# Order of the first loads, and early loads of the later x tiles, in a one-core transformer block

## The chip, the cores and the metric

The kernel runs on one core of a Trainium2 chip. The metric is the time of one execution in device microseconds; the smaller the better. The engines are named as in the profile: PE is TensorE's matrix multiplication and PEld its weight load, DVE is VectorE, ACT is ScalarE, POOL is GpSimd, and SP is the engine that issues nearly all transfers.

## The reference, cut to what matters

One block of a transformer over 1024 tokens of width 1024, in float32:

```python
x = x + _hybrid_mixer(_rms_norm(x, norm1_g), w_in, ...)      # two kinds of sparse attention
x = x + _memory_xattn(_rms_norm(x, norm2_g), mem, ...)       # cross attention over 256 memory rows
x = x + _sq_relu_mlp(_rms_norm(x, norm3_g), w_ff_in, w_ff_out)

def _rms_norm(x, g):
    return x * rsqrt(mean(x * x, axis=-1) + 1e-6) * g

# at the start of _hybrid_mixer, h being the normalised x
proj = h @ w_in                       # 1024 x 1760
c_q, c_kv, k_idx, w_idx, q_nsa, kv_nsa, g_nsa = split(proj)
q_d = rope(rms_norm(rms_norm(c_q) @ w_dsa_uq));  q_i = rope(rms_norm(c_q) @ w_idx_q)
k_d, v_d = split(rms_norm(c_kv) @ w_dsa_ukv)     # keys are normalised and rotated too
```

From `kv_nsa` come keys and values of three branches, one of them compressed over blocks of 32 tokens. The queries then attend, 128 at a time, to the top 256 keys of an index score, to compressed blocks, to selected blocks and to a window of 512.

## The kernel before, in words

Tokens are handled in eight tiles of 128 rows. `PARTS` makes two parts of them, tiles one to four and tiles five to eight. The **head** projects part 0 (`project(p1, 0, ...)`): each tile of x is loaded, normalised and transposed by `norm_T` (square on ACT with the sum of squares, a reciprocal root on DVE and POOL, the scaling by root and gain on DVE at line 290, the transposes on PE at line 277 into PSUM, evacuation by ACT and DVE), and then the columns of `w_in` are worked through in chunks of 256 by `gemm`. In the head x and the weights are split into a high and a low half, so that one product takes three matmuls (`load_w`, `split_w`; line 221 is the helper that issues a matmul). In the second part one float32 matmul takes their place (`load_whole`, line 268). `compress` makes the compressed keys and values. `k_prep` normalises and rotates the keys and transposes them (lines 460 to 480). `stage_q` copies projected queries from PSUM into a staging tile and stores them to DRAM (lines 404 and 406); `q_prep` reads them back for attention (line 559).

The **main phase** runs attention tile by tile (`attend`, with `scores`, whose rows of scores lie in the four-buffer tile `S`) beside a generator `fill`, which projects part 1 in the pool `p2`, then computes the memory keys, the output projection and the feed-forward layer of the first tiles. `together` fixes how the two are interleaved in the program. The **tail** finishes the feed-forward layer of the last four tiles.

On-chip memory is given out by pools. The pool `p1` serves the head and is closed before `p2`, which takes the same room; `at` lives from the start to the end of attention, and `aw` is opened after the head and holds attention's working tiles, `S` among them. A tag in a pool has a fixed number of buffers (`RINGS`), taken in turn: x tiles, the gain row, normalised rows, mask tables and compression weights share the five buffers of `x4` in `p1`, or the three in `p2`. The normalisation in `p2` writes its small results into `p2` as well.

The order of instructions on each engine is made by a list scheduler when the kernel is built: it takes what is ready by the modelled times, in the order of the program where several are ready. On the chip each engine then runs its own list in order and waits at semaphores. SP's transfers are such a list, too. Before the head begins, `build` issues, in this order, the identity, the tables of cosine and sine, three gains of queries, the gain of the cross attention, the two mask tables, and the positional rows of compression (`pe_stack`); only then `project` issues the gain of the first norm (line 340) and the x tiles (line 378).

Of the kernel before, what the change touches and what calls it, by code (L numbers as in the profile page):

```python
# [9 lines left out]
F32 = mybir.dt.float32  # L10
# [12 lines left out]
P = 128  # L23
# [10 lines left out]
KG = 2  # L34
NS = 4
G = 2
RINGS = {
    "p1": {"x4": 5, "st": 2, "relu": 4, "wraw": 4, "whi": 6, "wlo": 6, "c8": 4, "c4": 2, "kraw": 5, "pc": 2},
    "p2": {"x4": 3, "st": 1, "relu": 2, "whi": 4, "wlo": 4, "c8": 3, "c4": 1, "kraw": 4, "pc": 2},
    "dn": {"b4": 4, "h": 8, "relu": 2, "wraw": 2, "whi": 4, "wlo": 4},  # L40
# [129 lines left out]
def build(nc, tc, I, C, out):  # L170
# [114 lines left out]
    def norm_T(pool, x_t, gb, xs):  # L285
        ss = small(pool, "nss", 1)
        xn = ring(pool, "x4", [P, DM])
        s.activation(xn, x_t, AF.Square, accum_out=ss)
        r = rsqrt_of(pool, ss, DM, 1, "n")
        v.scalar_tensor_tensor(xn, x_t, r[:, 0:1], gb, op0=ALU.mult, op1=ALU.mult)  # L290
        to_T(pool, xn, xs, DM // P)
# [10 lines left out]

    def gemm(pool, xs, nk, nt, wsrc, chunks, consume):

        for ci, parts in enumerate(chunks):
            w = sum(n for _, n in parts)
            gr = []
            for k0 in range(0, nk, KG):
                kn = min(KG, nk - k0)
                srcs, o = [], 0  # L310
                for c0, n in parts:
                    srcs.append((lambda r, o=o, n=n: r[:, :, o:o + n],
                                 wsrc[k0 * P:(k0 + kn) * P, c0:c0 + n].rearrange("(k p) n -> p k n", p=P)))
                    o += n
                ws = load_w(pool, [P, kn, w], *srcs) if len(xs) == 2 else load_whole(pool, [P, kn, w], *srcs)
                gr += [[x[:, k, :] for x in ws] for k in range(kn)]
            for t in range(nt):
                pt = pst(TAGS[pool.name][0], [P, w])
                for k in range(nk):
                    if len(xs) == 1:  # L320
                        mm(pt, xs[0](t, k), gr[k][0], k == 0, k == nk - 1)
                        continue
                    wh, wl = gr[k]
                    xh, xl = xs[0](t, k), xs[1](t, k)
                    mm(pt, xh, wh, k == 0, False)
                    mm(pt, xh, wl, False, False)
                    mm(pt, xl, wh, False, k == nk - 1)
                consume(ci, t, pt)
                yield nk * (5 - len(xs)) * w / 2400.0
# [18 lines left out]

    cos = const("c_cos", [P, NT, 32], at)
    sin = const("c_sin", [P, NT, 64], at)  # L350
    qg = at.tile([P, 3, 64], F32, tag="qg", name="qg")
    nc.sync.dma_start(qg[:, 0, :], row(W["dsa_qn_g"]).to_broadcast([P, 64]))
    nc.sync.dma_start(qg[:, 1, :], row(W["nsa_qn_g"]).to_broadcast([P, 64]))
    nc.sync.dma_start(qg[:, 2, :], W["nsa_kn_g"][0:1].to_broadcast([P, 64]))
    v.tensor_scalar(qg[:, 0:2, :], qg[:, 0:2, :], -1.0, None, op0=ALU.mult)
    qgs = at.tile([P, 3, 64], F32, tag="qgs", name="qgs")
    v.tensor_copy(halves(qgs), swap(qg))
    xqg = bcast("xqg", row(W["xq_norm_g"]), 128)
    masks = const16("c_masks", [P, 640])
    window, causal = masks[:, 0:512], masks[:, 128:640]  # L360
    cmask = const16("c_cmask", [P, NT, 64])
    qraw = [[[dr.tile([P, n, 256], F32, tag=f"q{k}{t}{c}", name=f"q{k}{t}{c}") for c in range(2)] for t, n in PARTS]
# [7 lines left out]

    def project(pool, part, pe, st):
        t0, nt = PARTS[part]
        gb1 = gain(pool, W["norm1_g"])
        whole = part > 0
        _, xf, xt_of = xT(pool, nt, whole)
        for t in range(nt):
            x_t = ring(pool, "x4", [P, DM])
            nc.sync.dma_start(x_t, I["x"][0, (t0 + t) * P:(t0 + t + 1) * P, :])
            norm_T(pool, x_t, gb1, xt_of(t))
            yield 1.0  # L380
        cq = [ring(pool, "c8", [P, nt, 2, P], F32 if whole else F32R) for _ in xf]
        ckv = [ring(pool, "c4", [P, nt, P], F32 if whole else F32R) for _ in xf]
# [18 lines left out]
        def stage_q(k, c, t, pt):  # L401
            if t == 0:
                qst[:] = [ring(pool, "st", [P, nt, 256])]
            s.activation(qst[0][:, t, :], pt, AF.Copy)
            if t == nt - 1:
                nc.sync.dma_start(qraw[k][part][c], qst[0])
# [40 lines left out]

        def w_in(chunks, first):
            return gemm(pool, xf, DM // P, nt, W["w_in"], chunks,
                        lambda ci, t, pt: consume(ci + first, t, pt))  # L450

# [3 lines left out]
        def k_prep():  # L455
            for t in range(nt):
# [17 lines left out]
                for h0, hn in ((0, 4), (4, 2)):  # L474
                    p2 = pst("M", [P, hn, P])
                    for h in range(hn):
                        te.transpose(p2[:, h, :], kd[:, h0 + h, :, :].rearrange("p b d -> p (b d)"), ident)
                    dst = st["K"][:, h0:h0 + hn, T * P:(T + 1) * P]
                    s.activation(dst, p2, AF.Copy)
                    v.tensor_tensor(dst[64:128], p2[64:128], dst[64:128], op=ALU.subtract)  # L480
                yield 1.0

        KT += [ring(pool, "c8", [P, 2, nt * P + (0 if part else 16)]) for _ in range(2)]
        for kv in range(0 if part else 2):
            p3 = pe[:, kv, :].rearrange("p (a l) -> p a l", a=2)
            g.tensor_copy(KT[kv][0:64, :, nt * P:], p3[0:64])
            g.tensor_copy(KT[kv][64:128, :, nt * P:nt * P + 15], p3[64:128, :, 1:])
        yield from w_in([[(968, 256)]], 4)
        yield from w_in([[(0, 256)], [(256, 200), (1736, 24)]], 0)
# [172 lines left out]
    def scores(aw, qh, ql, K, kt0, nk, mask, gate):  # L662
# [518 lines left out]
    def fill():  # L1181
        for part in range(1, len(PARTS)):
            with tc.tile_pool(name="p2", bufs=1, reuse_waits="tile") as p2:
                yield from project(p2, part, pe, st)
            projected.append(part)
# [13 lines left out]
    together(attend(aw, st), rest, projected)  # L1199
    aw_pool.__exit__(None, None, None)  # L1200
    at_pool.__exit__(None, None, None)
    res_pool = tc.tile_pool(name="res", bufs=1, side="right", reuse_waits="tile")
# [34 lines left out]
```

## Time and profile before

| | us |
|---|---|
| median of 3 runs | 1802.85 (1801.54 to 1806.27) |
| the profiled execution | 1801.64 |
| its span in the profile | 1799.6 |
| mean granted TensorE clock | 0.977 of full speed |
| ACT busy | 1080.4 (60%) |
| DVE busy | 951.0 (53%) |
| POOL busy | 892.6 (50%) |
| moved by the queues | 193.80 MB, 108 GB/s in the mean |

The span is what the profile records, and the profiled execution's own time is 2.04 us longer. Busy shares are means over the whole span; the stages differ. Times in views of the profile count from the start of the span.

### The profile page before, as it was taken

The page shows a single profiled execution, that of the slowest core. Times are in us where ns is not written, and L with a number is a line of the kernel's source. Part 1 is how long each engine was busy: PE and PEld are TensorE (multiplying, and loading weights), DVE is VectorE, ACT ScalarE, POOL GpSimd, SP SyncE. Part 2 cuts the span into 40 slices and gives each one's busy share as a digit, 9 for nine tenths or more (in the row PEclk, how much of TensorE's full clock was granted, in tenths as well). Part 3 has the DMA queues.
Part 4 walks back from the last instruction along what each step waited for, and adds up shares of the span by engine and source line. Part 5 has one row for each costly group of instructions (what it writes and reads, how often), then busy time and mean ns, then how long its engine had stood idle before and what let it go on. Part 6 is the DMA issues. An engine that isn't in the chain of part 4 may idle for free.

```text
span 1799.6 us, 28055 instructions
## 1 busy us (share of the span) xinstructions
PE 1696.2 (94%) x9326; PEld 1457.3 (81%) x9326; DVE 951.0 (53%) x2381; ACT 1080.4 (60%) x2703; POOL 892.6 (50%) x1025
## 2 busy tenths in 40 slices
PE   5987999899989999999998999999999889999998
PEld 5986888688878777788886888887988878888887
DVE  4555757665873776365654555646524552222223
ACT  4444659797688579856896557994412543333333
POOL 2356647463551355568576576662211444444445
PEclk9997999999999999999999999999989899999999
DMA  6235221366336321222222122225375642333333
GB/s 193 74 119 150 71 76 58 109 197 177 99 107 192 98 63 42 70 71 79 61 67 83 55 71 67 67 75 187 108 245 158 209 118 84 96 94 98 96 118 107
DMA packets 176977, 193.80 MB, mean 108 GB/s; under 512 B 25664, under 2 KB 144192, under 8 KB 176832
## 3 DMA queue, kind: packets, MB, share of 16 engines
q1 hardware_dynamic: 168896, 181.52, 33.2%
q0 software_dynamic: 7936, 10.49, 2.2%
q8 instruction: 74, 1.21, 0.3%
q14 instruction: 71, 0.58, 0.1%
HBM read 170.98 MB, written 20.97 MB: 107 GB/s over the span
## 4 chain that ended last, share of the span: by engine, by line
PE 67%; DVE 9%; POOL 7%; ACT 5%; issue 5%; DMA 5%; SPq 1%; POOLq 0%; ACTq 0%; DVEq 0%
PE psD L221 48%; PE psS L221 8%; PE psPV L221 5%; PE psPT L698 4%; POOL wlo L252 3%; DMA wraw<-in_w_ff_in_dram 1%; PE psM L277 1%; ACT dmask L639 1%; DVE pl L239 1%; DVE S L681 1%; PE psPT L585 1%; ACT S L683 1%; ACT ph L238 1%; DMA qin<-q 1%; ACT whi L247 1%
## 5 line engine op out<-in xcount | busy, mean ns | idle before, releaser
L252 POOL TENSOR_TENSOR wlo<-wraw,whi 128x512 fp32r<-128x512 f32 (+1 forms) x225 | 309.5, 1380 | 266.7 <-ACT whi L247 263.0
L221 PE MATMUL psD<-whi,h 128*128 128x512 f32 x1024 | 340.7, 401 | 9.7 <-DVE b L1126 5.4
L247 ACT ACTIVATE whi<-wraw 128x512 fp32r<-128x512 f32 x321 | 200.7, 628 | 216.7 <-PE psD L221 156.4
L221 PEld LDWEIGHTS psD<-whi,h 128*128 128x128 f32 x1024 | 193.0, 190 | 55.2 <-DVE b L1126 8.8
L221 PE MATMUL psD<-xh,whi 128*128 128x512 f32 (+1 forms) x576 | 212.1, 372 | 1.2 <-ACT xh L238 0.8
L221 PE MATMUL psD<-xh,wlo 128*128 128x512 f32 (+1 forms) x576 | 212.9, 370 | 0.2 <-POOL wlo L252 0.2
L221 PE MATMUL psD<-xl,whi 128*128 128x512 f32 (+1 forms) x576 | 212.1, 370 | 0.0
L221 PE MATMUL psD<-wlo,h 128*128 128x512 f32 x512 | 203.2, 399 | 1.1 <-POOL wlo L252 1.1
L221 PE MATMUL psD<-whi,xh 128*128 128x256 f32 (+1 forms) x704 | 191.7, 353 | 4.3 <-ACT whi L247 3.2
L221 PE MATMUL psD<-wlo,xh 128*128 128x256 f32 (+1 forms) x704 | 191.3, 354 | 1.3 <-DMA wlo<-in_w_in_dram 0.7
L239 DVE TENSOR_TENSOR pl<-psPT,ph 128x512 fp32r<-128x512 f32 (+1 forms) x232 | 142.0, 620 | 80.1 <-ACT ph L238 77.4
L683 ACT ACTIVATE S<-S,mn 128x128 f32<-128x128 f32 (+7 forms) x192 | 142.6, 744 | 38.5 <-DVE mn L681 36.9
L688 POOL TENSOR_SCALAR S<-S,sums,gi 128x640 f32<-128x640 f32 (+7 forms) x128 | 107.0, 846 | 113.7 <-DVE sums L686 101.8
L252 DVE TENSOR_TENSOR wlo<-wraw,whi 128x512 fp32r<-128x512 f32 (+1 forms) x96 | 83.8, 873 | 148.8 <-ACT whi L247 148.5
L238 ACT ACTIVATE ph<-psPT 128x512 fp32r<-128x512 f32 (+1 forms) x232 | 122.7, 539 | 63.2 <-PE psPT L698 59.0
L221 PEld LDWEIGHTS psD<-wlo,xh 128*128 128x128 f32 x704 | 133.3, 194 | 13.4 <-ACT relu L416 1.2
L221 PEld LDWEIGHTS psD<-whi,xh 128*128 128x128 f32 x704 | 130.7, 194 | 14.2 <-ACT whi L247 3.6
L698 PE MATMUL psPT<-c_ident,S 128*128 128x128 f32 x816 | 131.4, 277 | 3.0 <-POOL S L688 1.6
L221 PEld LDWEIGHTS psD<-xh,whi 128*128 128x128 f32 x576 | 108.8, 189 | 19.3 <-ACT xh L238 1.6
L221 PEld LDWEIGHTS psD<-xh,wlo 128*128 128x128 f32 x576 | 109.0, 189 | 17.6 <-POOL wlo L252 0.9
L221 PEld LDWEIGHTS psD<-xl,whi 128*128 128x128 f32 x576 | 108.8, 189 | 17.1
L221 PE MATMUL psS<-K,qh 128*128 128x384 f32 (+3 forms) x288 | 112.7, 395 | 8.6 <-DVE mn L681 4.0
(282 smaller groups left out, 3863.7 us busy)
## 6 DMA issues: line engine op xcount, KB each, us to landing
wraw<-in_w_ff_in_dram SPq DMA_DIRECT2D x40, 512.0 KB, 4.0
wraw<-in_w_ff_out_dram SPq DMA_DIRECT2D x40, 512.0 KB, 3.9
wraw<-in_w_ff_in_dram SPq DMA_DIRECT2D x64, 256.0 KB, 2.7
wraw<-in_w_ff_out_dram SPq DMA_DIRECT2D x64, 256.0 KB, 2.7
whi<-in_w_out_dram SPq DMA_DIRECT2D x32, 256.0 KB, 3.6
wlo<-in_w_out_dram SPq DMA_DIRECT2D x32, 256.0 KB, 3.7
wraw<-in_w_in_dram SPq DMA_DIRECT2D x24, 256.0 KB, 3.7
q<-st SPq DMA_DIRECT2D x12, 512.0 KB, 2.6
```

The lines of the kernel that those rows point to most:

```text
L221: te.matmul(o, a, b, start=start, stop=stop)
L238: s.activation(hi, src, AF.Copy)
L239: v.tensor_tensor(lo, src, hi, op=ALU.subtract)
L247: s.activation(hi, raw, AF.Copy)
L252: (v if l == "v" else g).tensor_tensor(lo, raw, hi, op=ALU.subtract)
L277: te.transpose(pt[:, j, :], x_t[:, (c + j) * P:(c + j + 1) * P], ident)
L585: te.transpose(p2[:, h, :], qd[:, h, :, :].rearrange("p b d -> p (b d)"), ident)
L639: s.activation(mask, src, AF.Sign, bias=c, accum_out=over)
L681: v.tensor_tensor_reduce(out=dst, in0=sp, in1=m, scale=1.0, scalar=mn[:, 0:1] if i else 3e38, op0=ALU.add, op1=ALU.min, accum_out=low)
L683: s.activation(S, S, AF.Exp, bias=low, scale=-1.0, accum_out=sums[:, hh:hh + 1])
L688: g.tensor_scalar(Ss[hh], Ss[hh], sums[:, hh:hh + 1], 1.0 if gate is None else gate[:, hh:hh + 1], op0=ALU.mult, op1=ALU.mult)
L698: te.transpose(p2[:, j, hh, :], S[:, (c + j) * P:(c + j + 1) * P], ident)
```

## The change

The first transfer of the program is now x tile one; the identity, the gain of the first norm, and then the four weight groups of the first `w_in` chunk and x tiles two to four in turn follow it. Tiles two to four go into buffers of `S`, which lies in a pool of its own (`sp`), opened before `p1`. The tables, gains, masks and positional rows that stood ahead are issued after the normalisation of the four tiles. While `k_prep` runs in the head, x tiles five to eight are loaded into `S` buffers as well, each pinned behind the transfer traced before it on SP. In part 1 the normalisation takes these tiles instead of loading; it is given a priority as if it stood 300 places earlier in the program, its small results lie in `at`, and `x4` has five buffers in `p2`. In `stage_q` every second copy of the DSA and index queries (k = 0 and 2) is made by DVE instead of ACT. `gemm` takes the groups of its first chunk from its caller if they are loaded already; a new function `weights` holds the loading that stood in `gemm`.

```diff
+SOONER = 300
-    "p2": {"x4": 3, "st": 1, "relu": 2, ...
+    "p2": {"x4": 5, "st": 1, "relu": 2, ...
...
+    sp_pool = tc.tile_pool(name="sp", bufs=1, side="right", reuse_waits="tile")
+    srow = sp_pool.__enter__()
...
+    late = {"x": ring(p1, "x4", [P, DM])}
+    nc.sync.dma_start(late["x"], I["x"][0, 0:P, :])
     ident = const("c_ident", [P, P])
...
     def norm_T(pool, x_t, gb, xs):
-        ss = small(pool, "nss", 1)
+        ss = small(at, "nss", 1)
         xn = ring(pool, "x4", [P, DM])
         s.activation(xn, x_t, AF.Square, accum_out=ss)
-        r = rsqrt_of(pool, ss, DM, 1, "n")
+        r = rsqrt_of(at, ss, DM, 1, "n")
...
+    def weights(pool, xs, nk, wsrc, parts):
+        w = sum(n for _, n in parts)
+        for k0 in range(0, nk, KG):
...
+            ws = load_w(pool, [P, kn, w], *srcs) if len(xs) == 2 else load_whole(pool, [P, kn, w], *srcs)
+            for k in range(kn):
+                yield [x[:, k, :] for x in ws]
+
+    def gemm(pool, xs, nk, nt, wsrc, chunks, consume, begun=None):
         for ci, parts in enumerate(chunks):
             w = sum(n for _, n in parts)
...
+            gr = begun if ci == 0 and begun else list(weights(pool, xs, nk, wsrc, parts))
...
-    cos = const("c_cos", [P, NT, 32], at)
-    sin = const("c_sin", [P, NT, 64], at)
...
-    cmask = const16("c_cmask", [P, NT, 64])
...
+    ahead = {0: late["x"]}
...
+        begun = []
+        if not whole:
+            ws = weights(pool, xf, DM // P, W["w_in"], [(968, 256)])
+            for t in range(1, nt):
+                begun += [next(ws) for _ in range(KG)]
+                ahead[t] = small(srow, "S", L, bufs=NS)
+                nc.sync.dma_start(ahead[t], I["x"][0, t * P:(t + 1) * P, :])
+            begun += list(ws)
         for t in range(nt):
-            x_t = ring(pool, "x4", [P, DM])
-            nc.sync.dma_start(x_t, I["x"][0, (t0 + t) * P:(t0 + t + 1) * P, :])
-            norm_T(pool, x_t, gb1, xt_of(t))
+            if t0 + t in ahead:
+                x_t = ahead.pop(t0 + t)
+            else:
+                x_t = ring(pool, "x4", [P, DM])
+                load_x(x_t, t0 + t)
+            with tc.high_priority(offset=part * SOONER):
+                norm_T(pool, x_t, gb1, xt_of(t))
             yield 1.0
...
-            s.activation(qst[0][:, t, :], pt, AF.Copy)
+            if k != 1 and t % 2 == part:
+                v.tensor_copy(qst[0][:, t, :], pt)
+            else:
+                s.activation(qst[0][:, t, :], pt, AF.Copy)
...
+                if part == 0:
+                    ahead[4 + t] = small(srow, "S", L, bufs=NS)
+                    tc.keep_in_program_order(load_x(ahead[4 + t], 4 + t))
                 yield 1.0
...
-            S = small(aw, "S", L, bufs=NS)[:, :nk * P]
+            S = small(srow, "S", L, bufs=NS)[:, :nk * P]
...
-    pe = pe_stack()
     plan["w"] = PLAN_HEAD
-    drain(project(p1, 0, pe, st))
+    head = project(p1, 0, late, st)
+    for _ in range(PARTS[0][1]):
+        next(head)
+    cos = const("c_cos", [P, NT, 32], at)
+    sin = const("c_sin", [P, NT, 64], at)
...
+    cmask = const16("c_cmask", [P, NT, 64])
+    late["pe"] = pe_stack()
+    drain(head)
```

More of the change, by code (lines that the diff above doesn't have):

```diff
@@ L38 @@
     "p1": {"x4": 5, "st": 2, "relu": 4, "wraw": 4, "whi": 6, "wlo": 6, "c8": 4, "c4": 2, "kraw": 5, "pc": 2},
-    "p2": {"x4": 3, "st": 1, "relu": 2, "whi": 4, "wlo": 4, "c8": 3, "c4": 1, "kraw": 4, "pc": 2},
+    "p2": {"x4": 5, "st": 1, "relu": 2, "whi": 4, "wlo": 4, "c8": 3, "c4": 1, "kraw": 4, "pc": 2},
     "dn": {"b4": 4, "h": 8, "relu": 2, "wraw": 2, "whi": 4, "wlo": 4},
@@ L347, in gain2 @@
         return gs
-    cos = const("c_cos", [P, NT, 32], at)
-    sin = const("c_sin", [P, NT, 64], at)
[L351 to L360, printed above, removed]
-    cmask = const16("c_cmask", [P, NT, 64])
     qraw = [[[dr.tile([P, n, 256], F32, tag=f"q{k}{t}{c}", name=f"q{k}{t}{c}") for c in range(2)] for t, n in PARTS]
@@ L368, in build, with load_x, project @@
     xo_dr = [dr.tile([P, 512], F32, tag=f"xo{t}", name=f"xo{t}") for t in range(NT)]
-    def project(pool, part, pe, st):
+    ahead = {0: late["x"]}
+    def load_x(x_t, t):
+        return nc.sync.dma_start(x_t, I["x"][0, t * P:(t + 1) * P, :])
+    def project(pool, part, late, st):
         t0, nt = PARTS[part]
@@ L446, in consume, with w_in @@
                 split_ps(pt[:, 128:256].rearrange("p (a d) -> p a d", d=64), V[:, T, :, 0, :], V[:, T, :, 1, :])
-        def w_in(chunks, first):
+        def w_in(chunks, first, begun=None):
             return gemm(pool, xf, DM // P, nt, W["w_in"], chunks,
-                        lambda ci, t, pt: consume(ci + first, t, pt))
+                        lambda ci, t, pt: consume(ci + first, t, pt), begun)
         def consume_kv(ci, t, pt):
@@ L487, in project @@
             g.tensor_copy(KT[kv][64:128, :, nt * P:nt * P + 15], p3[64:128, :, 1:])
-        yield from w_in([[(968, 256)]], 4)
+        yield from w_in([[(968, 256)]], 4, begun)
         yield from w_in([[(0, 256)], [(256, 200), (1736, 24)]], 0)
@@ L1168, in build @@
         v.memset(st["cT"][kv], 0.0)
-    pe = pe_stack()
     plan["w"] = PLAN_HEAD
-    drain(project(p1, 0, pe, st))
+    head = project(p1, 0, late, st)
[3 more added lines that the diff above has]
+    sin = const("c_sin", [P, NT, 64], at)
+    qg = at.tile([P, 3, 64], F32, tag="qg", name="qg")
+    nc.sync.dma_start(qg[:, 0, :], row(W["dsa_qn_g"]).to_broadcast([P, 64]))
+    nc.sync.dma_start(qg[:, 1, :], row(W["nsa_qn_g"]).to_broadcast([P, 64]))
+    nc.sync.dma_start(qg[:, 2, :], W["nsa_kn_g"][0:1].to_broadcast([P, 64]))
+    v.tensor_scalar(qg[:, 0:2, :], qg[:, 0:2, :], -1.0, None, op0=ALU.mult)
+    qgs = at.tile([P, 3, 64], F32, tag="qgs", name="qgs")
+    v.tensor_copy(halves(qgs), swap(qg))
+    xqg = bcast("xqg", row(W["xq_norm_g"]), 128)
+    masks = const16("c_masks", [P, 640])
+    window, causal = masks[:, 0:512], masks[:, 128:640]
+    cmask = const16("c_cmask", [P, NT, 64])
+    late["pe"] = pe_stack()
+    drain(head)
     plan["w"] = PLAN_MAIN
@@ L1183, in fill @@
             with tc.tile_pool(name="p2", bufs=1, reuse_waits="tile") as p2:
-                yield from project(p2, part, pe, st)
+                yield from project(p2, part, late, st)
             projected.append(part)
```

19 lines of the change are left out of this document (8 added, 11 removed).

## The prediction

> **What bounds the kernel now.** I read the page first, then the busy times by stage, the chain that ended last, and the instructions in order of time around the two stages that stood out.
>
> ```profile
> span 1799.6 us, 28055 instructions
> ...
> PE 1696.2 (94%) x9326; PEld 1457.3 (81%) x9326; DVE 951.0 (53%) x2381; ACT 1080.4 (60%) x2703; POOL 892.6 (50%) x1025
> ```
>
> TensorE is busy 94% of the span, so time can be won almost only where it stands still. The stages (us; length, then busy time and count of PE, PEld, DVE, ACT, POOL; granted clock, DMA share, GB/s) say where:
>
> ```profile
> 0.00:30.00 30.00, 9.87 (x53) 9.36 (x54) 11.95 (x23) 11.39 (x20) 5.97 (x14) 1.00 0.66 207
> ...
> 20.00:30.00 10.00, 7.51 (x43) 7.52 (x44) 8.30 (x12) 7.98 (x16) 4.40 (x5) 1.00 0.83 271
> ...
> 30.00:131.00 101.00, 98.65 (x851) 97.23 (x849) 55.09 (x130) 51.04 (x149) 44.47 (x43) 1.00 0.36 102
> ...
> 131.00:172.00 41.00, 27.16 (x126) 22.64 (x126) 17.65 (x61) 16.24 (x48) 23.21 (x39) 0.71 0.48 153
> ...
> 170.00:300.00 130.00, 128.57 (x770) 114.06 (x769) 89.50 (x324) 89.98 (x334) 76.30 (x129) 1.00 0.27 70
> ...
> 172.00:1799.60 1627.60, 1560.56 (x8301) 1328.10 (x8300) 866.31 (x2169) 1001.70 (x2486) 818.94 (x931) 0.98 0.35 105
> ```
>
> In the dense head (30 to 131) one matmul costs 98.65 / 851 = 0.116 us. The first 30 us hold 53 matmuls, 6.1 us of work at that price: 23.9 us are lost. In the mixed stage 170 to 300 one costs 128.57 / 770 = 0.167 us; the 126 between 131 and 172 are then 21.0 us of work in 41: 20.0 us are lost, some in idling and some in the granted clock of 0.71. After 172, 1627.60 - 1560.56 = 67.0 us of idling are spread over the rest, which the change hardly touches. So the edits bear on two losses, 23.9 and 20.0 us. The chain of waits names what ends them (start us, us, what):
>
> ```profile
> 18.23 5.60 DMA x<-in_x_dram
> ...
> 133.22 5.50 DMA qin<-q
> ...
> 140.65 4.75 DMA wlo<-in_w_in_dram
> ```
>
> Both are chains of transfers.
>
> **The first loads.** Start us, us, engine, line, what; in brackets the idle time before and what ended it:
>
> ```profile
> 0.73 0.38 SPq L197 DMA_DIRECT2D c_ident<-in_c_ident_dram  x1
> ...
> 7.22 0.42 SPq L340 DMA_DIRECT2D x<-in_norm_g_dram  x1
> 7.77 0.35 SPq L378 DMA_DIRECT2D x<-in_x_dram  x1
> ...
> 13.83 1.06 ACT L288 ACTIVATE x<-x 128x1024 f32<-128x1024 f32 x1 [1.95 <-DMA x<-in_x_dram]
> ...
> 15.97 1.28 DVE L290 SCALAR_TENSOR_TENSOR x<-x,nr,x 128x1024 f32<-128x1024 f32 x1 [0.74 <-POOL nr L234]
> ...
> 17.31 1.97 PE L277 MATMUL psM<-c_ident,x 128*128 128x128 f32 x8 [5.69 <-DVE x L290]
> ...
> 22.48 0.58 PE L221 MATMUL psD<-whi,xh 128*128 128x256 f32 x1 [3.21 <-ACT whi L247]
> 22.59 0.34 SPq L378 DMA_DIRECT2D x<-in_x_dram  x1
> ```
>
> SP issues twelve transfers before the first rows of x, and the fourth x tile goes out only at 22.59, since its ring slot has to come free. The change issues x tile 0 first, then the identity, the gain, and weight groups and x tiles in turn, into the score room, which nobody holds. The landings:
>
> ```profile
> x<-in_x_dram SPq DMA_DIRECT2D x8, 512.0 KB, 5.3
> ...
> x<-in_norm_g_dram SPq DMA_DIRECT2D x2, 512.0 KB, 5.0
> ...
> wlo<-in_w_in_dram SPq DMA_DIRECT2D x12, 256.0 KB, 3.3
> ```
>
> ```profile
> DMA to landing us min/median/max: 3.6/5.3/6.0
> ```
>
> The last is line 378 alone. Up to the fourth x tile the order carries 5 x 512 + 64 + 3 x 256 = 3392 KB, 3.47 MB. At the 271 GB/s of 20 to 30 that is 12.8 us. The fastest landing, 3.6 us, less 1.9 us for its 0.52 MB leaves 1.7 us of fixed delay. The fourth tile lands at 0.73 + 1.7 + 12.8 = 15.2. From the square to the transposes tile 0 took 17.31 - 13.83 = 3.5 us, the transposes 1.97, and I allow 1.3 us for the two halves' split (the 128x512 copy further down takes 0.69); 24 matmuls add 2.8. The first chunk of `w_in` then ends at 24.8, and holds 96 matmuls and 32 transposes, 14.8 us of work: 10.0 us lost instead of 23.9, a gain of 13.9. I take 11, since ACT and DVE, already 8 of 10 us busy from 20 to 30, must do the same work in less time. At the mean 207 GB/s of the first 30 us the fourth tile lands 4.0 us later, which leaves 9.9. Behind it on SP go the displaced loads, 23 small ones, before the second chunk's weights: at the old pace, (7.22 - 0.73) / 12 = 0.54 us each, 12.4 us, so from about 5 to 17.5, landed at 20.8, before 24.8: hidden. If they go out slower and the cover is gone, up to 4 us more. Bounds of this term: -14 and -6.
>
> The moved tables (cos, sin, masks, gains, positional rows) are first needed by compression and key preparation inside the dense 101 us, which hides them. The four late x loads add 4 x 0.34 us on SP and 2.1 MB where the queues move 102 GB/s against 271 possible; behind them on SP stand weight loads, for which PE would wait at most those 1.4 us. I cost both at nothing.
>
> **The joint between head and second part.**
>
> ```profile
> 117.45 14.37 SPq L406 DMA_DIRECT2D q<-st  x5
> 131.91 0.38 SPq L340 DMA_DIRECT2D x<-in_norm_g_dram  x1
> 132.40 0.73 SPq L378 DMA_DIRECT2D x<-in_x_dram  x1
> ...
> 140.65 0.43 SPq L268 DMA_DIRECT2D wlo<-in_w_in_dram  x1
> ```
>
> ```profile
> 138.38 1.06 ACT L288 ACTIVATE x<-x 128x1024 f32<-128x1024 f32 x1 [6.91 <-DMA x<-in_x_dram]
> ...
> 165.71 1.06 ACT L288 ACTIVATE x<-x 128x1024 f32<-128x1024 f32 x1 [0.60 <-PE psM L277]
> ```
>
> ```profile
> 141.82 1.09 PE L277 MATMUL psM<-c_ident,x 128*128 128x128 f32 x4 [10.76 <-DVE x L290]
> ...
> 145.44 2.07 PE L221 MATMUL psD<-wlo,xh 128*128 128x256 f32 x4 [0.73 <-DMA wlo<-in_w_in_dram]
> ```
>
> ```profile
> SPq L397 <- DMA x<-in_x_dram: 1.4, 1, 1.4
> ```
>
> The second part's loads stand behind the head's last store of q on SP, though SP idled between those stores. The next pool change shows the same:
>
> ```profile
> 338.12 13.13 SPq L406 DMA_DIRECT2D q<-st  x3
> 351.35 1.22 SPq L346 DMA_DIRECT2D h<-in_mem_norm_g_dram  x2
> ```
>
> So I take it that nothing of a new pool is queued before the old one's last instruction; the raised priority then reorders only within the main phase, and the gain still goes out at 131.91. It lands 5.0 us later, at 136.9; the squares are over by then, because all four x tiles lie in memory; the 1.28 us scaling puts the transposes at 138.2 instead of 141.82: 3.6 us. The weights no longer stand behind an x issue (0.73) and SP's wait for its landing (1.4): 138.5 instead of 140.65, landed after 3.3 us at 141.8 instead of 145.44: 3.6 us too. Next late are these weights. Tiles five to eight then follow each other, where the last square now starts at 165.71. Of the 20.0 us lost, 7.2 of idling remain (131 to 138.2), about 2 of the 3.6 in which only transposes run, and about 4 of low clock: 0.71 over 41 us stands for 11.9 us, and I keep a third, since later x tiles no longer thin out the stage. That makes 13.2, a gain of 6.8; I take 6. Ends: -3.6 (only the first shift is kept) and -10 (half the loss). With the S slots held by x, the first score row waits for tile five's scaling on DVE; behind it on DVE stand query preparation and softmax, whose q rows are loaded after the gain anyway: nothing.
>
> The Trainium skill, "TensorE: Matmul & The Clock Gate", part 1, says that the clock halves after about 3.4 us of idling and needs about 3.4 us of sustained work to return. By that rule the low clock after the remaining gap would cost about 1.7 us, not 4, and the sum would be 2 us lower. The trace here disagrees: a mean of 0.71 over 41 us means more than one such window.
>
> **Staging copies.** Half of the DSA and index query copies go from ACT to DVE.
>
> ```profile
> L221 PE MATMUL psD<-whi,c 128*128 128x256 f32 x33 | 8.4, 384 | 1.8 <-ACT st L404 1.8
> ...
> L404 ACT ACTIVATE st<-psD 128x256 f32<-128x256 f32 x25 | 9.0, 373 | 4.1 <-DMA q<-st 2.6 <-PE psD L221 1.4
> ...
> L283 DVE COPY xh<-psM 128x512 f32<-128x512 f32 x4 | 2.7, 686 | 2.1 <-PE psM L277 2.0
> ```
>
> In the second part PE waits 1.8 us for these ACT copies: 0 to -1.8, I take -1. In the head 8 of them join DVE's key preparation; at 0.69 us each, too dear since that is the double width, they cost at most 5.5 us, and nothing while PE has other work: +1.
>
> **Sum:** -11 - 6 - 1 + 1 = -17 us. The profiled execution took 1801.64 us (span 1799.6 and 2.04 around it), so 1784.6; the median of the runs, 1802.85, is 1.2 above it: 1785.8.
>
> **Rivals.** *Half of it.* ACT and DVE, not the loads, limit the first chunk, so that only the head start of x counts (6 us), and the joint keeps 3.6: 1793. For it speak the 8.30 and 7.98 busy us of 20 to 30; against it that they start idle now. 0.2.
>
> *The raised priority reaches across the joint.* The four tiles are scaled before the head ends and the joint's loss shrinks by 14: -25, 1778. For it speaks that ACT has 50 us free in the head; against it the order of SP at both pool changes. 0.05.
>
> *The gain is given back.* What PE wins it waits for later, because ACT's chain of index masks sets the pace of the first attention tiles: no change, 1803. Against it: 128.57 of 130 us of PE busy from 170 to 300. 0.09.
>
> *Slower: attention stands behind the scaling.* Before, only tile five was scaled ahead of attention's first query preparation; now all four are, on ACT, DVE and the one PSUM buffer of transposes. If nothing of a tile overlaps, that is 1.06 + 1.28 + 2 x (1.09 + 0.69) = 5.9 us, and 17.7 for the three new ones. If from there attention's own chain and not PE sets the pace, the joint gives no gain but this delay: -11 + 17.7 = +6.7, 1809.6. It decides once more than 16.4 us of the delay reach the end. The low granted clock and thin counts of 131 to 172 speak for a chain there, the full PE after 170 against it. 0.06.
>
> **How the numbers follow.** A measurement of this kernel tells about 0.3% from no change, 5.4 us. The sum's own case has 0.6; its bounds are -14 - 10 - 1.8 = -25.8, 1777.0, and -6 - 3.6 + 5.5 = -4.1, 1798.7, where four bounds would have to meet. Faster: 0.6 + 0.2 + 0.05 = 0.85; same 0.09; slower 0.06. The range 1776 to 1798 holds the first three cases; it leaves out the other two, 0.15, and about 0.05 of tails.
>
> **What would show it.** Right: the first transposes at about 9 us instead of 17.31, the first 30 us with over 130 matmuls, the head's last store some 11 us earlier, then about 6.5 us until the transposes and 10 to 11 until the first weights, with squares of tiles five to eight back to back. Wrong: small table loads on SP ahead of the second chunk's weights with PE waiting for them at 20 to 30 us; scaling already before the head's end; or a stage after 172 whose idle time has grown beyond 67 us, which no term here holds.

## The result, and the profile after

The changed kernel takes 1834.96 us in the median of 4 runs (1833.96 to 1837.42), beside 1803.44 us for the kernel before (4 runs): a ratio of 1.0176, with a 95% interval of 1.0158 to 1.0193. It is slower by 1.8%, and the forecast of 1785.8 us misses by 49 us. The profiled execution took 1837.42 us; the page of it begins

```profile
span 1835.7 us, 28055 instructions
...
PE 1711.8 (93%) x9326; PEld 1471.0 (80%) x9326; DVE 949.0 (52%) x2397; ACT 1078.9 (59%) x2687; POOL 882.0 (48%) x1025
```

Work and count are the same 9326 matmuls; 1835.7 - 1799.6 = 36.1 us more of span are 1711.8 - 1696.2 = 15.6 us in which the same matmuls took longer, and 20.5 us more of idling. The busy times by stage of the changed kernel, its stages cut at its own marks (the head's last store of q goes out at 126.4 instead of 131.5):

```profile
0.00:30.00 30.00, 17.85 (x120) 16.30 (x120) 13.36 (x27) 13.85 (x25) 6.16 (x11) 1.00 0.74 223
20.00:30.00 10.00, 9.01 (x73) 8.42 (x72) 5.28 (x13) 3.32 (x7) 1.29 (x1) 1.00 0.83 209
30.00:126.00 96.00, 93.49 (x782) 92.29 (x782) 53.81 (x134) 44.65 (x138) 43.12 (x45) 1.00 0.43 124
126.00:167.00 41.00, 30.63 (x168) 26.38 (x169) 22.05 (x75) 19.91 (x60) 25.39 (x45) 0.83 0.61 153
...
167.00:1835.70 1668.70, 1569.87 (x8258) 1336.05 (x8256) 859.80 (x2162) 1000.45 (x2466) 807.33 (x925) 0.97 0.33 101
```

Both edited stages got better: 120 matmuls instead of 53 in the first 30 us, and in the 41 us after the head 168 instead of 126 at a clock of 0.83 instead of 0.71. At 167 the changed kernel is 5 us and 168 - 126 = 42 matmuls ahead (7.0 us at 0.167), about 12 us. The last line gives all of it back four times over: idling after this point is 1668.70 - 1569.87 = 98.8 us instead of 67.0, and 43 matmuls fewer than in the kernel before (8258 against 8301) are busy 9.3 us longer. The loss after 167 is 31.8 + 9.3 + 43 x 0.167 = 48 us.

It does not lie in one place. The first long wait of PE that the kernel before does not have stands at the pool change, where part 1's pool `p2` gives way to that of the memory's work. Waits of PE between 300 and 360 us (total, times, longest), the kernel before first:

```profile
PE psD L221 <- ACT st L404: 3.7, 2, 1.9
...
PE psS L221 <- ACT ir L607: 0.4, 1, 0.4
```

```profile
PE psS L224 <- ACT ir L628: 11.0, 1, 11.0
PE psD L224 <- DVE st L420: 3.5, 3, 2.0
```

The index relu `ir` is ACT's copy of an index score out of PSUM, without which PE cannot go on. The chain of waits of the changed kernel shows what it stood behind:

```profile
339.36 6.49 DMA b<-in_mem_dram
345.87 1.15 ACT xh L301 x2
347.02 0.49 ACT ir L628
```

These are ACT's instructions in order of time (start, us, what; in brackets the idle time before): the kernel before, and then the changed one.

```profile
343.58 0.59 ACT L607 ACTIVATE ir<-psS 128x512 f32<-128x512 f32 x1
...
356.13 0.59 ACT L607 ACTIVATE ir<-psS 128x512 f32<-128x512 f32 x1
359.68 1.06 ACT L296 ACTIVATE xh<-b 128x1024 f32<-128x1024 f32 x1
```

```profile
345.87 1.06 ACT L301 ACTIVATE xh<-b 128x1024 f32<-128x1024 f32 x1 [6.31 <-DMA b<-in_mem_dram]
346.83 0.19 ACT L301 ACTIVATION_READ_ACCUMULATOR xh<-b 128x1 f32 x1
346.93 1.06 ACT L628 ACTIVATE ir<-psS 128x512 f32<-128x512 f32 x2
```

In the kernel before, attention's index relus come first and the square of the memory's rows (`norm_T2` in `memory`, the work that follows part 1 in `fill`) after them: ACT has attention's work while the rows are on their way (issued at 353.16), and the square starts at 359.68 with no idle time before it. In the changed kernel the square stands first in ACT's list and waits 6.31 us for its rows, loaded only at 339.36; the relus, ready, wait behind it, and PE behind them. So the order on ACT is another one, far from any edited line. The stores of projected q and of attention's output (`o<-oc`; duration, first and last start) show what else has moved, before and after:

```profile
L712 SPq DMA_DIRECT2D o<-oc x64: 575/586/609, 173.6 to 1305.8; - x64
L406 SPq DMA_DIRECT2D q<-st x12: 319/320/343, 105.9 to 350.9; - x12
```

```profile
L733 SPq DMA_DIRECT2D o<-oc x64: 574/586/997, 166.1 to 1340.6; - x64
L424 SPq DMA_DIRECT2D q<-st x12: 319/322/545, 101.5 to 337.1; - x12
```

Part 1's projection ends 13.8 us earlier, and attention ends 34.8 us later. From attention's last store to the end of the span it is 1799.6 - 1305.8 = 493.8 us before and 495.1 after: attention's last tile sets the end, and the filling work's lead is worth nothing there. Attention's 4th, 12th and 20th stores, before and after:

```profile
197.86 3.88 SPq L712 DMA_DIRECT2D o<-oc  x2
...
277.20 0.59 SPq L712 DMA_DIRECT2D o<-oc  x1
...
382.79 0.59 SPq L712 DMA_DIRECT2D o<-oc  x1
```

```profile
193.40 10.39 SPq L733 DMA_DIRECT2D o<-oc  x3
...
282.94 0.59 SPq L733 DMA_DIRECT2D o<-oc  x1
...
401.47 0.59 SPq L733 DMA_DIRECT2D o<-oc  x1
```

4.5 us early, then 5.7 late, then 18.7 late: attention gives up 10 us while part 1 gets ahead, 13 more over the pool change at 337, and the rest later.

### The profile page after: what moved, and what is told of

The parts are those of the page before. It is cut to its first block, busy times and chain, and to the rows that moved or that the text cites. A ratio compares the mean times of both kernels' runs of the same rounds, so it can differ in the third digit from the quotient of the medians.

```text
span 1835.7 us, 28055 instructions
## 1 busy us (share of the span) xinstructions
PE 1711.8 (93%) x9326; PEld 1471.0 (80%) x9326; DVE 949.0 (52%) x2397; ACT 1078.9 (59%) x2687; POOL 882.0 (48%) x1025
## 4 chain that ended last, share of the span: by engine, by line
PE 74%; DVE 6%; ACT 6%; DMA 6%; POOL 4%; issue 3%; SPq 1%; POOLq 0%; ACTq 0%; DVEq 0%
PE psD L224 52%; PE psS L224 10%; PE psPV L224 5%; PE psPT L719 4%; PE psM L282 1%; POOL wlo L257 1%; ACT dmask L660 1%; DMA wraw<-in_w_in_dram 1%; PE psPT L606 1%; DMA whi<-in_w_out_dram 1%; DMA relu<-xo 1%; ACT S L704 1%; ACT whi L252 1%; DVE pl L244 1%; DVE S L702 1%
## 5 line engine op out<-in xcount | busy, mean ns | idle before, releaser
L257 POOL TENSOR_TENSOR wlo<-wraw,whi 128x512 fp32r<-128x512 f32 (+1 forms) x225 | 305.0, 1361 | 286.7 <-ACT whi L252 282.5
L257 DVE TENSOR_TENSOR wlo<-wraw,whi 128x512 fp32r<-128x512 f32 (+1 forms) x96 | 80.0, 834 | 144.4 <-ACT whi L252 144.2
L224 PEld LDWEIGHTS psD<-whi,xh 128*128 128x128 f32 x704 | 131.4, 195 | 15.2 <-DVE h L244 1.9
L224 PEld LDWEIGHTS psD<-wlo,xh 128*128 128x128 f32 x704 | 132.4, 194 | 13.8 <-DMA wlo<-in_w_in_dram 3.0
```

The source lines that it names most:

```text
L224: te.matmul(o, a, b, start=start, stop=stop)
L257: (v if l == "v" else g).tensor_tensor(lo, raw, hi, op=ALU.subtract)
```

## Experiments

The theories at the start: **A**, part 1 gets ahead of attention, and what follows part 1 then stands in the lists ahead of attention's work; **B**, the kernel before has a lucky order in its main phase, and any edit that redraws the list costs some 30 us; and, for each part of the change, that this part costs. Ratios are to the kernel before on the same chip, with 95% intervals. "Ahead" below is counted in the order of ACT's instructions: how many of the score rows' exponentials and index relus stand ahead of part 1's last staging copy (58 and 13 in the kernel before, 54 and 10 in the changed one).

**The change cut in parts.** *only_start* keeps the order of the first loads (with the pool of `S` and the small results in `at`) and leaves out the rest.

```diff
-SOONER = 300
+SOONER = 0
...
-    "p2": {"x4": 5,
+    "p2": {"x4": 3,
...
-            if k != 1 and t % 2 == part:
-                v.tensor_copy(qst[0][:, t, :], pt)
-            else:
-                s.activation(qst[0][:, t, :], pt, AF.Copy)
+            s.activation(qst[0][:, t, :], pt, AF.Copy)
...
-                if part == 0:
-                    ahead[4 + t] = small(srow, "S", L, bufs=NS)
-                    tc.keep_in_program_order(load_x(ahead[4 + t], 4 + t))
```

> Only the new order of the first loads: the late loads of tiles five to eight, the raised priority, DVE's staging copies and the larger ring of the second part are taken out of the changed kernel. Theory A (the second part now runs ahead of attention, and attention, left behind, empties later stages): the joint is as before, so the late part is harmless here; the head ends some 5 us earlier as in the changed kernel, 1795 to 1802. Theory B (any edit in the head makes the list scheduler draw a new order of the main phase, good or bad by chance): the main phase moves by 10 us and more in either direction, 1785 to 1830, with more or less than 67 us of idling after the joint.

1792.52 us, ratio 0.996 (0.9944 to 0.9976). The start is a gain, the main phase keeps most of the old order, and the gain lasts: attention's last store at 1295.4, 10.4 us earlier. The time lies a little below A's range, and this version beats both kernels.

*only_late* is the kernel before with the late loads, the raised priority, the new pool and the ring of five, without the start and the DVE copies.

```diff
-    "p2": {"x4": 3,
+    "p2": {"x4": 5,
...
+            with tc.high_priority(offset=part * 300):
...
+                if part == 0:
+                    ahead[4 + t] = small(srow, "S", L, bufs=NS)
+                    tc.keep_in_program_order(load_x(ahead[4 + t], 4 + t))
```

> The kernel before with only the late loads of tiles five to eight, the raised priority of their normalisation, and what they need (the pool of score rows, small results in the lasting pool, five buffers in the second part); first loads and staging as before. Theory A: the joint shrinks by about 7 us and the loss after it is all there: 1828 to 1842. Theory B: a third draw, anywhere from 1785 to 1835.

1834.88 us, 1.0181 (1.0137 to 1.0225): the whole loss, without the start. *no_priority* is the changed kernel with `SOONER = 0`.

> The changed kernel with the normalisation of tiles five to eight at its own place in the program (offset 0 instead of 300). Theory A: tiles six to eight wait for their turn behind attention's first tile again, the second part is less far ahead, and about half of the loss goes: 1810 to 1822. Theory B: a new draw, without relation to how far ahead the second part is.

1834.77 us, 1.0181 (1.0137 to 1.0224), and every engine has the changed kernel's order of instructions: the raised priority does nothing, and the half of the loss that A put on it is not there. *swap_gains* is the kernel before with two neighbouring loads of gain rows in the head exchanged.

```diff
-        nc.sync.dma_start(cqg, ...)
         nc.sync.dma_start(ckvg, ...)
+        nc.sync.dma_start(cqg, ...)
```

> The kernel before with two neighbouring small loads (the gains of 256 and 128 columns) issued in the other order, 0.4 us apart and both landed long before use: no work is added or moved. Theory A: 1803, within 3 us. Theory B in its strong form (every edit draws a new order): a time more than 5 us from 1803 is possible; if it is 1803 within 3 us, small edits don't redraw the main phase.

1802.07 us, 1.0008 (0.999 to 1.0026). A small edit of the head redraws nothing: but for these loads on SP, every engine keeps its order.

**Which half of the late part.** *ring5_alone* changes one number of the kernel before; *late_ring3* is *only_late* with the ring of three; *start_late_ring3* is the changed kernel with the ring of three and all copies on ACT.

```diff
-    "p2": {"x4": 3,
+    "p2": {"x4": 5,
```

> The kernel before with one number changed: five buffers instead of three for x4 in the second part. Theory R (the larger ring lets the second part's projection run ahead, and the order of the main phase that follows from it is the bad one): slower by 25 to 35 us, 1826 to 1836, with PE waiting about 10 us for ACT when the memory rows are loaded. Theory X (x tiles five to eight lying in memory at the joint is what does it, the ring is only room): 1798 to 1806.

> The kernel with only the late loads (34 us slower than before), with three buffers of x4 in the second part again. Theory R: the joint keeps its gain and the main phase its old course: 1792 to 1800. Theory X: slow as with five, 1828 to 1838. If any change at the joint redraws the order by chance, something between.

> The changed kernel with three buffers of x4 in the second part and all staging copies on ACT: first loads and late loads stay. Theory R: both gains add, 8.5 from the start and 5 to 8 from the joint: 1786 to 1792, faster than both kernels. Theory X: 1825 to 1835.

1844.66 us, 1.0228 (1.0198 to 1.0258); 1838.39, 1.0193 (1.0149 to 1.0238); 1829.93, 1.0146 (1.0117 to 1.0176). Two more buffers, with no x loaded early, cost 41 us; the late loads without the buffers cost 35; together they cost no more. So neither the transfers of the late loads nor the score rows' room is needed for the loss: *ring5_alone* has neither. R, which puts all of it on the ring, falls by the second and third, and X, which puts it on the x tiles lying ready, by the first. What the three share is that part 1 works further ahead (its last store of q goes out at 337.8, 341.4 and 331.9 us instead of 350.9), and that PE stands still for 10 to 12.5 us at the pool change, for the memory's scaled rows or for an index relu (waits of PE, 300 to 360 us; one line each, in the order above):

```profile
PE psM L277 <- DVE relu L300: 12.5, 1, 12.5
```

```profile
PE psS L223 <- ACT ir L621: 10.1, 1, 10.1
```

```profile
PE psS L224 <- ACT ir L625: 10.8, 1, 10.8
```

*memory_square_later* pins the memory rows' squares on ACT behind what the text puts ahead of them, and puts 12 units of attention there.

```diff
+                yield 12.0
...
+        tc.keep_in_program_order(sq)
```

> The changed kernel, with the squares of the two memory tiles on ACT pinned behind the attention work traced ahead of them and 12 units of attention put there, so that they don't stand in ACT's list ahead of an evacuation that PE waits for (11.0 us, and 6.9 us of halved clock behind it). If that stall is the main cause: 1815 to 1820. If attention being late is the cause and the stall one sign of it: 1826 to 1835, with waits elsewhere.

1890.26 us, 1.0481 (1.0423 to 1.0539). The time lies far outside both ranges. The amount was wrong: the filling work fell 75 to 100 us behind, and PE still waited 8.0 us for an index relu. Nothing follows for A or B, but that the other side, fill late, is dearer still.

**Holding part 1 back, and taking the stall away.** *part1_held_back* has the start, the late loads and the raised priority, the ring of three, and part 1's copies pinned.

```diff
-PACES = (1.35, 1.35, 1.35, 1.75, 1.75)
+PACES = (2.3, 1.35, 1.35, 1.75, 1.75)
...
-            s.activation(qst[0][:, t, :], pt, AF.Copy)
+            i_ = s.activation(qst[0][:, t, :], pt, AF.Copy)
+            if part:
+                tc.keep_in_program_order(i_)
```

> The changed kernel with its start, its late loads into the score rows' room and its raised priority, with the ring of three again, and with one thing added: part 1's 24 copies of the projected rows of q (all on ACT) are each kept behind what the program's text puts ahead of them on ACT, and the text's first pace is 2.3 instead of 1.35, so that the head's second half ends beside the same attention work as in the kernel before (in ACT's list 60 of the score rows' exponentials and 15 index relus stand ahead of part 1's last copy; 58 and 13 in the kernel before, 54 and 10 in all the slow kernels). Theory A (part 1, once its rows are there, runs ahead of the attention, and the memory rows' squares then stand in ACT's list ahead of the index relus): the order is back, so the loss goes and the start's gain stays: 1788 to 1803 us, no wait of PE for an index relu over 3 us between 300 and 360 us. Theory B (the kernel before has a lucky order in its main phase, and any new draw costs some 30 us): 1820 to 1840 us. Theory C (the late loads themselves cost, by their transfers or their rows' room): 1825 to 1840 us.

1802.70 us, 0.9995 (0.9981 to 1.0008), 27 us below *start_late_ring3*, from which it differs in these lines alone. Part 1 ends late and attention is back in its place; PE's wait for an index relu between 300 and 360 us:

```profile
L732 SPq DMA_DIRECT2D o<-oc x64: 574/581/1112, 170.4 to 1308.6; - x64
L423 SPq DMA_DIRECT2D q<-st x12: 319/320/382, 100.9 to 360.3; - x12
```

```profile
PE psS L224 <- ACT ir L627: 2.0, 1, 2.0
```

So the loss belongs to the order of the main phase, not to the loads, and C falls; with late loads and an order in which attention is not overtaken the loss is gone. But the time lies at the upper end of A's range: of the start's gain nothing is left either.

*memory_without_transfer* is the changed kernel with the memory's values left out:

```diff
-            nc.sync.dma_start(x_t, I["mem"][0, t * P:(t + 1) * P, :])
+            nc.gpsimd.memset(x_t, 0.5)
```

> The changed kernel with the two loads of the memory's rows replaced by GpSimd memsets of the same tiles (the memory's values are left out), so that the squares in ACT's list wait for no transfer. It prices the one stall of 11 us at 336 us with what follows from it. Theory A as first put (this stall begins the loss): the wait for the index relu falls from 11.0 to under 4 us, the attention's store 19 comes 8 to 14 us sooner, and the time is 1805 to 1822 us. Theory B (any draw costs): 1828 to 1840 us. If the stall goes and the time stays within 5 us of 1835, the attention's lag comes from part 1 having taken engine time from it, and not from the stall.

1822.68 us, 1.0109 (1.0087 to 1.013): 12.3 us less than the changed kernel, just outside A's range. The wait for the relu is gone, but another one of PE at the same pool change, for the scaling of the memory's rows, takes most of its place:

```profile
PE psM L282 <- DVE relu L305: 7.3, 1, 7.3
```

What the 12 us are is not shown. The index relu behind the memory's squares comes no sooner (347.35 us against 346.93), and attention's 19th store, which A wanted 8 to 14 us sooner, goes out at 386.3 against 384.9; PE, ACT and DVE have another order from some 342 to 348 us on, so that these 12 us may be a new draw. (From attention's last store, at 1317.3, to the end it is 509.7 us here, where the kernels before and after have 493.8 and 495.1.)

*start_and_staging* is *only_start* with the DVE copies; *pace_attention_first* is the kernel before with a first pace of 1.2.

> The changed kernel's start and its DVE copies of every second staged tile alone: no late loads, no raised priority, ring of three. In ACT's list 57 exponentials and 13 index relus stand ahead of part 1's last copy, as in the kernel before. Theory A: the start's gain stays and the staging is worth what the prediction gave it in the head and a little in the main phase: 1788 to 1796 us. Theory B (any new draw of the main phase costs some 30 us; this one's order differs from the kernel before's in the main phase, as the copies change engines): 1815 to 1830 us.

> The kernel before with one number changed: the first pace 1.2 instead of 1.35, which puts more attention ahead of the filling work in the program's text. The main phase's list is drawn anew (PE's differs from the kernel before's from 200 us on), but part 1 does not run ahead: 58 exponentials and 13 index relus stand ahead of part 1's last copy on ACT, as in the kernel before. Theory A: 1798 to 1812 us. Theory B (any new draw costs some 30 us): 1820 to 1845 us.

1805.76 us, 1.0006 (0.9994 to 1.0019), and 1810.07 us, 1.0032 (1.0018 to 1.0046). Both keep attention in its place (57 or 58 exponentials, 13 relus ahead). The second is a weaker test than was expected: by the tiles that the instructions write and read, PE, ACT, DVE and POOL keep the order of the kernel before until some 831 us, and 986 of PE's 9326 places differ after that. The first has another order than *only_start* from 327 us of PE on (3977 places). Neither it nor *part1_held_back* (4027 places, against the kernel before) loses 30 us, so B falls as stated; but the first is above *only_start* by some 8 us by the two ratios, and the second 6 us above the kernel before. A new draw costs some 6 to 8 us here, and A's range for the first is missed. In the profiled runs most of the first's excess over *only_start* lies behind attention: its last store goes out 3.7 us later (1299.1 against 1295.4), and from there to the end it takes 504.4 us against 495.3.

**What made the held version good.** *part1_held_less* is *part1_held_back* with a pace of 2.6, *pace_without_pins* the same with 2.3 but without the pins.

```diff
-PACES = (2.3, 1.35, 1.35, 1.75, 1.75)
+PACES = (2.6, 1.35, 1.35, 1.75, 1.75)
```

> The version that held part 1 back, with one number changed: its first pace 2.6 instead of 2.3, the pinned copies kept. In ACT's list 54 exponentials and 10 index relus stand ahead of part 1's last copy, as in the slow kernels, instead of 60 and 15. Theory A (what matters is how much attention stands ahead of part 1's end): the loss is back, 1822 to 1840 us, with a wait of PE for an index relu of over 6 us between 300 and 360 us. Theory D (the pins keep part 1 in a good order whatever the pace): 1798 to 1808 us.

> The version that held part 1 back with its pins left out and its first pace of 2.3 kept: 54 exponentials and 10 index relus ahead of part 1's last copy on ACT. Theory A: 1822 to 1840 us. Theory E (the pace of 2.3 as such made the difference): 1798 to 1808 us.

1817.9 us, 1.0077 (1.0049 to 1.0105), and 1836.99 us, 1.0189 (1.0162 to 1.0215). PE's longest waits between 300 and 360 us are, in this order,

```profile
PE psS L224 <- ACT ir L627: 4.5, 1, 4.5
```

```profile
PE psM L282 <- DVE relu L305: 12.0, 1, 12.0
```

The pace alone does not help (E falls); with the pins it does (the pins at the old pace were not run). The less part 1 is held back, the later attention ends: part 1's last store goes out at 360.3, 340.1 and 332.1 us in the held, the less held and the free version, and attention's last store at 1308.6, 1319.1 and 1347.1. That is A's direction in three steps, but 1817.9 lies between the ranges of A and D: the count of instructions ahead is not the whole measure. Nor is the end of part 1: in *late_ring3* its last store goes out at 341.4, later than in the less held version, and the time is 20 us longer.

**Where this leaves the cause.** Shown: the loss is the order of the main phase, it comes with either edit that lets part 1 work ahead, it needs neither early transfers nor the score rows, and holding part 1 back takes it away. Not shown: what in that order costs the 32 us. The stall at the pool change is no full account, since it does not tell the good order from the bad: by 360 us PE has run 2062 matmuls in the kernel before, 2045 in the changed one and 2038 in *part1_held_back*, which loses nothing in the end. They part after it (the kernel before, the changed one, *part1_held_back*):

```profile
360.00:720.00 360.00, 336.07 (x1918) 289.56 (x1919) 243.63 (x688) 284.43 (x776) 163.94 (x231) 0.98 0.41 122
```

```profile
360.00:720.00 360.00, 326.91 (x1813) 282.47 (x1812) 231.41 (x666) 266.79 (x723) 146.10 (x215) 0.95 0.36 110
```

```profile
360.00:720.00 360.00, 335.67 (x1903) 290.85 (x1902) 237.89 (x692) 282.11 (x763) 159.07 (x229) 0.96 0.43 126
```

105 matmuls fewer are 18 us at the 336.07 / 1918 = 0.175 us of the first row, lost in many small gaps and half-clock stretches; the rest follows until attention's end. That each of these follows from attention's lateness is argued, not shown, and some 6 to 8 us of the loss may be the price of any new draw.

## Why the prediction was wrong, point by point

**The first loads: right in kind, mis-sized.** Forecast -11, measured 131.5 - 126.4 = 5.1 us at the head's last store, in *only_start* 4.9. The first transposes start at 10.15 instead of 17.31, where about 9 was expected, and the first 30 us hold 120 matmuls, not over 130:

```profile
10.15 1.97 PE L282 MATMUL psM<-c_ident,x 128*128 128x128 f32 x8 [10.15 <-DVE x L295]
```

The transfers came as computed: the fourth x tile landed at 15.06 us, where 15.2 was expected. The cover of the displaced small loads failed. They were to go out from 5 to 17.5 us; they went out from 8.68 to 21.92 (SP, and behind them the second chunk's weights; then ACT):

```profile
8.68 0.33 SPq L200 DMA_DIRECT2D c_cos<-in_c_cos_dram  x1
...
21.92 0.43 SPq L412 DMA_DIRECT2D pc<-in_idx_k_ln_b_dram  x1
22.77 1.49 SPq L262 DMA_DIRECT2D wraw<-in_w_in_dram  x3
```

```profile
27.32 0.63 ACT L252 ACTIVATE whi<-wraw 128x512 fp32r<-128x512 f32 x1 [4.17 <-DMA wraw<-in_w_in_dram]
28.79 0.63 ACT L252 ACTIVATE whi<-wraw 128x512 fp32r<-128x512 f32 x1 [0.84 <-DMA wraw<-in_w_in_dram]
...
36.16 0.58 ACT L252 ACTIVATE whi<-wraw 128x448 fp32r<-128x448 f32 x1 [2.94 <-DMA wraw<-in_w_in_dram]
```

That the stretch took 13.2 us, near the 12.4 of the text, is luck: there are 21 loads and not 23, and the old pace was 0.59 us (6.49 us for eleven steps) and not 0.54. ACT stood 4.17 + 0.84 + 2.94 = 8.0 us for weights that came behind them. PE lost far less by it; its only waits for ACT between 20 us and the head's end are

```profile
PE psM L455 <- ACT pe L1172: 1.3, 1, 1.3
PE psM L455 <- ACT relu L452: 1.0, 1, 1.0
```

or 2.3 us, within the 4 that the text had named for this risk. The step of this term that failed is the price of the matmuls. The text took all that the first 30 us fall short of 0.116 us per matmul as time that an earlier start wins back. Of the 23.9 us lost before, 30 - 9.87 = 20.1 were idling, and 9.87 - 6.1 = 3.8 were matmuls that took longer than 0.116. In the changed kernel 30 - 17.85 = 12.2 us are idling, 8 less, but the slow matmuls are still there: 17.85 - 120 x 0.116 = 3.9. So 16.1 us are lost, where the sum had 10.0. Of the gain of 7.8 at 30 us, some 3 go in the dense stage, whose 782 matmuls took 93.49 / 782 = 0.120 us instead of 0.116; why, no run shows. The bound of -6 did not hold what was left.

**The joint: right.** Transposes 6.5 us after the head's end and first weights 10 to 11 after it were expected; they come 7.0 and 12.6 us after 126.0, the weights some 2 us late, and the squares follow one another:

```profile
133.04 1.09 PE L282 MATMUL psM<-c_ident,x 128*128 128x128 f32 x4 [7.08 <-DVE x L295]
...
138.57 2.07 PE L224 MATMUL psD<-wlo,xh 128*128 128x256 f32 x4 [2.64 <-DMA wlo<-in_w_in_dram]
```

```profile
126.28 1.05 ACT L293 ACTIVATE x<-S 128x1024 f32<-128x1024 f32 x1
...
129.39 1.04 ACT L293 ACTIVATE x<-S 128x1024 f32<-128x1024 f32 x1
```

Gained there: 42 matmuls or 7.0 us, forecast 6. The step after it failed: that the lead of part 1 is a lead of the kernel. It was read from a PE that was full from 170 to 300, from which work done early seemed to be work saved; the end, though, is set by attention, whose stores lost in the same stage what part 1 won.

**"Which the change hardly touches": the failed step.** The 67.0 us of idling after 172 became 98.8 after 167. This was the last sign named under what would make the prediction wrong, and no term, no rival and no bound held it. The text described a scheduler that takes what is ready, and then added up an order that stays. It looked for what is queued behind the late loads, on SP and at the joint, and not for what stands behind the *end* of part 1, 200 us on.

**The ring of five** had no term at all. Alone it costs 41 us.

**The raised priority:** "reorders only within the main phase" was still too much; it reorders nothing. The rival in which it reaches across the joint falls.

**Staging:** -1 and +1 were forecast; with the start it costs some 8 us by its new draw (their ratios are 1.0006 and 0.996; the times, 1805.76 against 1792.52 us, are from two chips), and PE's wait for the copies between 300 and 360 us stayed (3.7 before, 3.5 after).

**The slower rival** had the side and one condition right, that attention's own chain sets the pace. Its place, the scaling at the joint, and its size, +6.7 us, were not: attention is still 4.5 us early at its 4th store. "The gain is given back" by ACT's chain of index masks comes nearer in place, as the relus of the index scores are what PE waits for, but by a square put ahead of them and not by the masks, and with four times the gain given back.

## What to carry to other kernels

Where a list scheduler makes the order, an edit that makes one stream of work ready earlier, even two more buffers, is a new order for everything beside it; before summing, ask which stream sets the end, and what follows the hurried stream in the in-order lists when it finishes early. An instruction that waits for a transfer holds back what is queued behind it on its engine (6.31 us of ACT here, and 11.0 of PE behind it), so look at the next pool change and not only at the edited lines. A part that gains and leaves most of the order as it was (here the first loads, 0.4%) is best taken alone, and each edit of a bundle timed for itself.

## What the runs showed of the hardware

Small gaps of PE can cost clock as well as idling. The changed kernel's busy times around two of its stretches at half clock:

```profile
129.00:142.70 13.70, 6.33 (x19) 4.74 (x20) 7.14 (x12) 2.54 (x6) 7.17 (x10) 0.50 0.77 232
```

```profile
455.00:463.50 8.50, 5.15 (x29) 3.71 (x27) 6.98 (x26) 4.01 (x12) 0.70 (x1) 1.00 0.42 128
463.50:473.70 10.20, 8.99 (x39) 8.14 (x39) 6.85 (x22) 5.24 (x16) 3.28 (x6) 0.50 0.29 74
473.70:490.00 16.30, 16.19 (x95) 13.75 (x95) 9.51 (x34) 7.81 (x22) 5.51 (x8) 1.00 0.31 100
```

After 8.50 - 5.15 = 3.35 us of idling, spread over 8.5 us in pieces of 1.9 us at most, the clock was at half for 10.2 us, although PE was busy for 8.99 of them. At the 16.19 / 95 = 0.170 us of a matmul in the last row, these 39 would have taken 6.6 us. So some 2.4 us went to the clock, for gaps that look harmless in a list of waits; this is an estimate, since the kinds of matmuls differ from row to row. At the joint the half clock lasted 13.7 us, but with 6.33 us of work in it that cost 3.2 us, where the prediction had 4. The Trainium skill, "TensorE: Matmul & The Clock Gate", part 1, has the clock halve after an idle window of about 3.4 us and return after one of about 3.4 us of sustained work. The lengths here agree with such a window, being multiples of it (10.2 is three, 13.7 four). The rest agrees less plainly: no single idle time between 455 and 463.50 was over 1.9 us, and the return took three windows, at 88% busy. Whether gaps as small as these keep work from counting as sustained, no run here shows.
